# A transformer trunk on one core: the row-scaling after a transpose moves to one engine, and the weight ring grows by a slot

## The chip, the core and the metric

The kernel runs on one core of one Trainium2 chip. A core has a matrix engine (TensorE, PE in the profile), whose weight loads are listed apart (PEld), a vector engine (VectorE, DVE), an activation engine (ScalarE, ACT), a general engine (GpSimd, POOL) and a queue engine (SyncE, SP) that issues most transfers. Each engine works through its own instructions in order and waits on semaphores. The metric is the device time of one execution in microseconds, the median of the runs shown; lower is better.

## The reference

Two layers, each of three sub-layers on a sequence of 256 rows of width 1024, all in float32. Each sub-layer norms its input, scales and shifts it by vectors that come from a conditioning vector `c` (adaLN), and adds its gated result to `x`:

```python
for l in range(2):
    mod = silu(c) @ ada_w[l] + ada_b[l]               # 9 vectors of 1024
    sh1, sc1, g1, sh2, sc2, g2, sh3, sc3, g3 = split(mod, 9)
    h = rms_norm(x, norm_ffn1[l]) * (1 + sc1) + sh1
    x = x + 0.5 * g1 * swiglu(h, ffn1_w_in[l], ffn1_w_out[l])     # 1024 -> 2 x 2816 -> 1024
    h = rms_norm(x, norm_mix[l]) * (1 + sc2) + sh2
    x = x + g2 * token_mix(h, ...)                    # gMLP heads beside top-k attention heads
    h = rms_norm(x, norm_ffn2[l]) * (1 + sc3) + sh3
    x = x + 0.5 * g3 * swiglu(h, ffn2_w_in[l], ffn2_w_out[l])
return rms_norm(x, final_norm)
```

## The kernel before, in words

The 256 rows are two blocks of 128, b = 0 and b = 1. There are six phases in a row: ffn1, mix, ffn2 of layer 0, then of layer 1. The five borders between them are called T1 to T5 here, in order of time (T1: ffn1 to mix of layer 0; T2: mix to ffn2; T3: ffn2 to the next layer's ffn1; T4 and T5 as T1 and T2, in layer 1).

Every matrix product is made of three fp32r matmuls: each operand is split into a high part and the rest (`hi`, `lo`), and hi·hi, hi·lo and lo·hi are added up in a PSUM bank (`mm3`, L488). Weights come from HBM in pieces of 128x1024 float32 into a ring of `NRAW` raw tiles (`raw`, one SP transfer each). ScalarE then copies a piece to `whi` (L455), and VectorE subtracts that from the raw piece to make `wlo` (L456); `whi` and `wlo` live in a ring of `NB` slots. The function `pump` does this for the next piece of a fixed list; a slot is free again when block b = 1 has used it (`release`), a raw tile when its piece is converted. Between the weights stand pieces of `ada_w`, which are multiplied by `c` and added up in `aacc`: the first on ScalarE (L435), the others on VectorE (L440).

The program's order is fixed when the kernel is built: the Python code walks through the work in items (one weight piece for one block), and after each item runs deferred work and calls `pump`. Each engine's queue is that order. In a phase, block 0 is up to `LAG` = 6 items ahead of block 1. So at a border block 0 already multiplies for the new phase while block 1 ends the old one:

- Block 0's last products of the old phase are added to `x` (`update`, L539 and L541), squared and summed (L502), the root taken on POOL (L512), the rows scaled (L516), and, some items later, transposed on TensorE (L733) by `norm_T`.
- `norm_T` reads the transposed rows from PSUM, a bank of 4 tiles of 128x128 for each half h of the width, and applies scale A and shift B, which are per-partition columns after the transpose: one instruction a tile. Then `split` makes `hThi` (ScalarE, L534) and `hTlo` (VectorE, L535) of each half.
- Block 1 then goes the same way: its `update` stands on VectorE behind block 0's split and behind two weight conversions, and its transposes are placed after four items of block 0 in the new phase. TensorE waits there until block 1's rows are scaled (L516).

The lines around the change are

```python
if h < YH:
    S.activation(y[:, k, :], ps[:, q * P:(q + 1) * P], AF.Identity, bias=B, scale=A)      # L527
else:
    V.tensor_scalar(y[:, k, :], ps[:, q * P:(q + 1) * P], A, B, op0=ALU.mult, op1=ALU.add)  # L529
```

and, for both halves, `for fn in [norm_T(b, l2, i2, h) for h in range(2)]: fn()` (L556 to L558): both halves are scaled first, and then both are split.

In a mix phase, block 0's first product (`idx`) is taken from PSUM on ScalarE (L774), rotated on VectorE (`rope`, L696 to L701), one column block copied on ScalarE (L779) and transposed on TensorE (L733 on `idx`). Later `sgu_out` makes `u` on VectorE (L954), which TensorE transposes too. POOL loads two small tables of each layer by transfers that it issues itself; the one for the gMLP (L738, used at L745) is the largest.

Of the kernel before, what the change touches and what calls it, by code (L numbers as in the profile page):

```python
# [20 lines left out]
KF = DFF // P  # L21
DEPTH = 2
EPS = 1e-6
NB = 10
LEADJ = 8
LAG = 6
NRAW = 7
HOLD = 3
TAIL = 3
VX = 188  # L30
# [30 lines left out]
F1 = 62  # L61
ADA0_ACT = 1
COL_D = 2
YH = 1
TRL = 5
XPOS = 0
WLEAD = 0
# [30 lines left out]
def trunk(ctx, tc, x_in, c_in, pos_in, ada_w, ada_b, norm_ffn1, ffn1_w_in, ffn1_w_out,  # L98
# [6 lines left out]
    small = ctx.enter_context(tc.tile_pool(name="small", bufs=2))  # L105
    rawp = ctx.enter_context(tc.tile_pool(name="rawp", bufs=NRAW))
    hlp = ctx.enter_context(tc.tile_pool(name="hlp", bufs=NB))
    aap = ctx.enter_context(tc.tile_pool(name="aap", bufs=2))
# [201 lines left out]
    def defer(n, fn):  # L310
        pend.append([n, fn])
# [15 lines left out]
    def dma_fill():  # L327
        while dp[0] < len(seq):
# [5 lines left out]
            else:  # L334
                if n_r[0] - n_rd[0] >= NRAW:
                    break
# [75 lines left out]
    def pump(quota=2, force=False):  # L412
# [3 lines left out]
        while sp[0] < len(seq) and quota > 0:  # L416
# [8 lines left out]
            if e["k"] == "w" and not force and len(W) - wcur[0] >= lead[0]:  # L425
                break
            if need and r >= NB and not ring[r - NB]:
                assert not force, (r, ring[r - NB:], wcur, [q[0] for q in pend])
                break
# [36 lines left out]
    wcur = [0, 0]  # L466
    lead = [NB]

# [49 lines left out]
    def norm_T(b, l, i, h):  # L518
# [4 lines left out]
        for q in range(4):  # L523
            k = h * 4 + q
            A, B = ab[:, l, i - 1, 0, k:k + 1], ab[:, l, i - 1, 1, k:k + 1]
            if h < YH:
                S.activation(y[:, k, :], ps[:, q * P:(q + 1) * P], AF.Identity, bias=B, scale=A)  # L527
# [641 lines left out]
    for pi, (kind, l, i, n) in enumerate(phases):  # L1169
        with ExitStack() as es:  # L1170
# [28 lines left out]
            def both(stop):  # L1199
                while cnt[1] < stop:  # L1200
                    if cnt[0] < stop and cnt[0] - cnt[1] <= LAG:
                        item(0)
                        if pi == len(phases) - 1 and cnt[0] == n - 10:
                            fin_g[0] = vecp.tile([P, D], F32, name="vec", tag="vec")
                            nc.sync.dma_start(fin_g[0], bcast_row(final_norm, D))
                    else:
                        item(1)
            if kind == "f":
                both(n - KF)
                lead[0] = LEADJ  # L1210
                for q, _ in enumerate(joint_gen(env)):
# [6 lines left out]
                    if i == 1 and q == 4:  # L1218
                        sgu_prep(l, env)
                        sguT[l] = env["sgu_T"]  # L1220
                        defer(6, env["sgu_fin"])
                lead[0] = NB
            both(n)
# [29 lines left out]
```

## Time and profile before

| | us |
|---|---|
| median of 3 runs | 1018.31 (1015.11 to 1019.42) |
| the profiled execution's own time | 1017.07 |
| its span, first to last instruction | 1015.3 |
| TensorE busy | 983.5 (97%) |
| VectorE busy | 775.9 (76%) |
| ScalarE busy | 539.0 (53%) |
| POOL busy | 19.8 (2%) |

The chain of work that ended last is 84% TensorE, 9% VectorE, 3% ScalarE. The span is what the profile's views cover; the execution's own time is 1.77 us longer. A TensorE that is busy for a whole stretch can only be helped by fewer or shorter matmuls; where it stands idle, the row that follows names what it waited for. So the views to read are the waits of TensorE, and then, for each wait, the order of time on VectorE and ScalarE ahead of it.

### The profile page before, as it was taken

What the parts mean: (1) busy time and instruction counts of PE and PEld (TensorE: products, weight loads), DVE (VectorE), ACT (ScalarE), POOL (GpSimd) and SP (SyncE); (2) the same over time, 40 slices, a digit from 0 to 9 for tenths busy, and PEclk for the clock granted to TensorE, in tenths of its full rate; (3) what the DMA queues carried; (4) which work ended last, traced back from release to release, by engine and by line L of the source; (5) the groups of instructions that cost most, each with busy time, mean ns of one, the idle gap of its engine ahead of it and who ended that gap; (6) DMA issues with size and microseconds to landing.
All of it is one profiled execution on the core that took longest, in us unless ns stands there. A gap on an engine that the chain in (4) does not pass through costs nothing.

```text
span 1015.3 us, 16506 instructions
## 1 busy us (share of the span) xinstructions
PE 983.5 (97%) x6352; PEld 871.8 (86%) x6352; DVE 775.9 (76%) x1095; ACT 539.0 (53%) x832; POOL 19.8 (2%) x39
## 2 busy tenths in 40 slices
PE   5999999998999999999999999999999999999997
PEld 3699998887778799998878999987778879999886
DVE  3898988877997888887679798885879787566554
ACT  5575454446576645543456555534667766445341
POOL 4000000000000000000000000000000000000000
PEclk9999999999999999999999999999999999999999
DMA  9989899867664598878758899896555547665631
GB/s 328 340 309 339 316 380 346 317 203 230 192 188 146 168 346 313 313 273 289 273 161 289 341 330 353 320 343 193 157 147 156 154 146 259 250 218 188 217 116 42
DMA packets 109775, 253.40 MB, mean 250 GB/s; under 512 B 8499, under 2 KB 26981, under 8 KB 109697
## 3 DMA queue, kind: packets, MB, share of 16 engines
q1 hardware_dynamic: 108864, 251.20, 71.9%
q8 instruction: 50, 0.82, 0.3%
q0 software_dynamic: 544, 0.63, 0.2%
q10 hardware_dynamic: 288, 0.52, 0.1%
q14 instruction: 29, 0.23, 0.1%
HBM read 251.27 MB, written 1.05 MB: 249 GB/s over the span
## 4 chain that ended last, share of the span: by engine, by line
PE 84%; DVE 9%; ACT 3%; issue 2%; POOL 1%; DMA 1%; SPq 0%; POOLq 0%; ACTq 0%; DVEq 0%
PE bank L489 13%; PE bank L672 13%; PE bank L674 13%; PE bank L676 13%; PE bank L491 13%; PE bank L490 13%; PE bank L733 3%; DVE wlo L456 2%; DVE x L541 1%; ACT whi L455 1%; DVE xm L539 1%; PE bank L1047 1%; POOL rstd L512 1%; DVE aacc L1053 1%; DMA x<-in_x_dram 1%
## 5 line engine op out<-in xcount | busy, mean ns | idle before, releaser
L456 DVE TENSOR_TENSOR wlo<-raw,whi 128x1024 fp32r<-128x1024 f32 (+1 forms) x328 | 392.4, 1212 | 111.7 <-ACT whi L455 110.9
L455 ACT ACTIVATE whi<-raw 128x1024 fp32r<-128x1024 f32 (+1 forms) x328 | 334.4, 1045 | 217.4 <-PE bank L491 136.3
L672 PE MATMUL bank<-hThi,whi 128*128 128x256 f32 x1152 | 321.0, 279 | 0.0
L674 PE MATMUL bank<-hTlo,whi 128*128 128x256 f32 x1152 | 319.6, 277 | 0.0
L676 PE MATMUL bank<-hThi,wlo 128*128 128x256 f32 x1152 | 319.6, 277 | 0.0
L676 PEld LDWEIGHTS bank<-hThi,wlo 128*128 128x128 f32 x1152 | 217.6, 189 | 0.0
L672 PEld LDWEIGHTS bank<-hThi,whi 128*128 128x128 f32 x1152 | 216.3, 188 | 0.3
L674 PEld LDWEIGHTS bank<-hTlo,whi 128*128 128x128 f32 x1152 | 216.3, 188 | 0.3
L489 PE MATMUL bank<-whi,hThi 128*128 128x512 f32 (+1 forms) x384 | 154.5, 402 | 1.8 <-ACT hThi L1083 1.8
L491 PE MATMUL bank<-whi,hTlo 128*128 128x512 f32 (+1 forms) x384 | 149.0, 388 | 1.9 <-DVE hTlo L486 1.3
L490 PE MATMUL bank<-wlo,hThi 128*128 128x512 f32 (+1 forms) x384 | 147.6, 384 | 0.0
L440 DVE SCALAR_TENSOR_TENSOR aacc<-raw,ccol,aacc 128x1024 f32<-128x1024 f32 x112 | 143.1, 1278 | 0.0
L489 PE MATMUL bank<-whi,aThi 128*128 128x512 f32 (+1 forms) x374 | 142.3, 381 | 0.0
L490 PE MATMUL bank<-wlo,aThi 128*128 128x512 f32 (+1 forms) x374 | 141.2, 377 | 0.0
L491 PE MATMUL bank<-whi,aTlo 128*128 128x512 f32 (+1 forms) x374 | 141.0, 377 | 0.0
L489 PEld LDWEIGHTS bank<-whi,hThi 128*128 128x128 f32 x384 | 72.3, 188 | 19.8 <-issue 3.2
L491 PEld LDWEIGHTS bank<-whi,hTlo 128*128 128x128 f32 x384 | 72.1, 188 | 19.4 <-DVE hTlo L486 3.0
L490 PEld LDWEIGHTS bank<-wlo,hThi 128*128 128x128 f32 x384 | 72.3, 188 | 13.2 <-issue 0.5
L491 PEld LDWEIGHTS bank<-whi,aTlo 128*128 128x128 f32 x374 | 70.3, 188 | 13.3
L489 PEld LDWEIGHTS bank<-whi,aThi 128*128 128x128 f32 x374 | 70.4, 188 | 12.7
L490 PEld LDWEIGHTS bank<-wlo,aThi 128*128 128x128 f32 x374 | 70.4, 188 | 12.4
L681 ACT ACTIVATE xm<-bank 128x256 f32<-128x256 f32 x72 | 25.4, 379 | 62.5 <-PE bank L676 62.5
(150 smaller groups left out, 675.3 us busy)
## 6 DMA issues: line engine op xcount, KB each, us to landing
raw<-in_ffn_w_in_dram SPq DMA_DIRECT2D x176, 512.0 KB, 5.2
raw<-in_ada_w_dram SPq DMA_DIRECT2D x128, 512.0 KB, 5.7
raw<-in_ffn_w_out_dram SPq DMA_DIRECT2D x88, 512.0 KB, 5.3
raw<-in_mix_w_in_dram SPq DMA_DIRECT2D x40, 512.0 KB, 3.9
sraw<-in_ada_w_dram SPq DMA_DIRECT2D x32, 256.0 KB, 6.6
raw<-in_mix_w_out_dram SPq DMA_DIRECT2D x16, 512.0 KB, 3.6
vec<-in_ada_b_dram SPq DMA_DIRECT2D x6, 512.0 KB, 6.1
raw<-in_mix_w_in_dram SPq DMA_DIRECT2D x8, 324.0 KB, 3.0
```

The lines of the kernel that those rows point to most:

```text
L440: V.scalar_tensor_tensor(aacc, e["raw"], ccol[:, j:j + 1], aacc, op0=ALU.mult, op1=ALU.add)
L455: S.activation(hi[:, :n], src, AF.Copy)
L456: V.tensor_tensor(lo[:, :n], src, hi[:, :n].bitcast(F32), op=ALU.subtract)
L489: T.matmul(ps, ahi, whi, start=first, stop=False)
L490: T.matmul(ps, ahi, wlo, start=False, stop=False)
L491: T.matmul(ps, alo, whi, start=False, stop=last)
L512: G.tensor_tensor(r, ms, mhalf, op=ALU.pow)
L672: T.matmul(o, wh[:, kk, sl], ahi, start=first, stop=False, skip_group_check=True)
L674: T.matmul(o, wh[:, kk, sl], alo, start=False, stop=False, skip_group_check=True)
L676: T.matmul(o, wl[:, kk, sl], ahi, start=False, stop=k == KD - 1, skip_group_check=True)
L681: S.activation(a, acc[j][:, :256], AF.Silu)
L733: T.transpose(ps[:, i * P:(i + 1) * P], src(i), ident)
```

## The change: three constants and a smaller scratch

`YH` goes from 1 to 2, so that the second half's four tiles (L529 on VectorE) become four more of L527 on ScalarE, for each block at each of the five borders: 40 VectorE instructions become 40 of ScalarE. `NB` goes from 10 to 11 and `NRAW` from 7 to 8. The scratch that the software transfers of POOL use shrinks to 4096 bytes a partition, which pays for the two slot tiles and the raw tile.

```diff
-NB = 10
+NB = 11
-NRAW = 7
+NRAW = 8
-YH = 1
+YH = 2
-    nc = _bacc.Bacc("TRN2", target_bir_lowering=False, num_devices=1)
+    nc = _bacc.Bacc("TRN2", target_bir_lowering=False, num_devices=1,
+                     dynamic_dma_scratch_size=4096)
```

ScalarE's queue at T2, from the end of block 0's norm to block 1's squares: `xm_107` are block 0's rows, `xm_108` block 1's. Before:

```order
L455 ACTIVATE whi<-raw 128x1024 x2
L527 ACTIVATE xm_107<-bank_85,ab 128x128 x4
L534 ACTIVATE hThi<-xm_107 128x512 x2
L455 ACTIVATE whi<-raw 128x1024 x2
L502 ACTIVATE xm_108,ss<-x_106 128x512 x2
```

and with the change:

```order
L455 ACTIVATE whi<-raw 128x1024 x2
L527 ACTIVATE xm_107<-bank_85,ab 128x128 x4
L527 ACTIVATE xm_107<-bank_79,ab 128x128 x4
L534 ACTIVATE hThi<-xm_107 128x512 x2
L455 ACTIVATE whi<-raw 128x1024 x2
L502 ACTIVATE xm_108,ss<-x_106 128x512 x2
```

Four instructions have come in between the transposed rows and the two weight conversions behind them; nothing else has moved. VectorE's queue at the same place, from block 0's scaled rows to block 1's update, before:

```order
L516 TENSOR_SCALAR xm_107<-x_105,rstd 128x512 x2
L486 TENSOR_TENSOR hTlo<-bank_83,hThi 128x512
L456 TENSOR_TENSOR wlo<-raw,whi 128x1024 x2
L529 TENSOR_SCALAR xm_107<-bank_79,ab 128x128 x4
L535 TENSOR_TENSOR hTlo<-xm_107,hThi 128x512 x2
L456 TENSOR_TENSOR wlo<-raw,whi 128x1024 x2
L539 SCALAR_TENSOR_TENSOR xm_108<-bank_81,vec 128x512
```

and with the change:

```order
L516 TENSOR_SCALAR xm_107<-x_105,rstd 128x512 x2
L486 TENSOR_TENSOR hTlo<-bank_80,hThi 128x512
L456 TENSOR_TENSOR wlo<-raw,whi 128x1024 x2
L535 TENSOR_TENSOR hTlo<-xm_107,hThi 128x512 x2
L456 TENSOR_TENSOR wlo<-raw,whi 128x1024 x2
L539 SCALAR_TENSOR_TENSOR xm_108<-bank_82,vec 128x512
```

The row of L529 is gone; the two conversions ahead of block 1's update (L539) are still there. The other four borders read the same way on both engines. VectorE's queue at T1, from block 1's scaled rows to the rotation of block 0's `idx`, before:

```order
L516 TENSOR_SCALAR xm_108<-x_106,rstd 128x512 x2
L456 TENSOR_TENSOR wlo<-raw,whi 128x1024 x2
L529 TENSOR_SCALAR xm_108<-bank_82,ab 128x128 x4
L535 TENSOR_TENSOR hTlo<-xm_108,hThi 128x512 x2
L456 TENSOR_TENSOR wlo<-raw,whi 128x1024
L696 TENSOR_TENSOR rt<-idx,sinT 128x5x8
L698 TENSOR_TENSOR rt<-idx,sinT 128x5x8
L700 TENSOR_TENSOR idx<-idx,cosT 128x5x16
L701 TENSOR_TENSOR idx<-idx,rt 128x5x16
L440 SCALAR_TENSOR_TENSOR aacc<-raw,ccol,aacc 128x1024
```

and with the change:

```order
L516 TENSOR_SCALAR xm_108<-x_106,rstd 128x512 x2
L456 TENSOR_TENSOR wlo<-raw,whi 128x1024 x2
L535 TENSOR_TENSOR hTlo<-xm_108,hThi 128x512 x2
L440 SCALAR_TENSOR_TENSOR aacc<-raw,ccol,aacc 128x1024
L456 TENSOR_TENSOR wlo<-raw,whi 128x1024
L696 TENSOR_TENSOR rt<-idx,sinT 128x5x8
L698 TENSOR_TENSOR rt<-idx,sinT 128x5x8
L700 TENSOR_TENSOR idx<-idx,cosT 128x5x16
L701 TENSOR_TENSOR idx<-idx,rt 128x5x16
```

Besides the row of L529, one `ada_w` step (L440) has come from behind the rotation to ahead of it: with one slot and one raw tile more, the list is one piece further at every point. In the mix phase of layer 1 there are no `ada_w` pieces, and at T4 only the row of L529 goes. TensorE's rows around the five borders, are the same in both programs, and so is the order in which SP issues its transfers, but for the load of the last norm's weights, which comes one piece later.

## Rows read from the trace of the kernel before

**Rows 1.** Busy time of each engine in one stretch (start:end, length, PE, PEld, DVE, ...).

```profile
52.00:206.00 154.00, 154.00 (x1119) 144.90 (x1120) 135.91 (x172) 80.95 (x104) 0.00 (x0) 1.00 0.92 336
```

**Rows 2.** Waits of TensorE: who waited for whom, total us, times, longest.

```profile
PE bank L733 <- DVE xm L516: 14.0, 8, 3.6
...
PE bank L733 <- DVE u L954: 1.5, 1, 1.5
```

**Rows 3.** Timeline at T2: start, us, engine, line, what [idle before <- releaser].

```profile
331.07 1.51 ACT L527 ACTIVATE xm<-bank,ab 128x128 f32<-128x128 f32 x4 [1.81 <-PE bank L733]
...
332.61 1.16 ACT L534 ACTIVATE hThi<-xm 128x512 fp32r<-128x512 f32 x2
...
333.28 1.29 DVE L535 TENSOR_TENSOR hTlo<-xm,hThi 128x512 fp32r<-128x512 f32 x2 [0.38 <-ACT hThi L534]
...
333.67 1.99 ACT L455 ACTIVATE whi<-raw 128x1024 fp32r<-128x1024 f32 x2
...
334.75 2.36 DVE L456 TENSOR_TENSOR wlo<-raw,whi 128x1024 fp32r<-128x1024 f32 x2 [0.18 <-ACT whi L455]
...
341.50 0.88 DVE L516 TENSOR_SCALAR xm<-x,rstd 128x512 f32<-128x512 f32 x2 [0.73 <-POOL rstd L512]
```

**Rows 4.** Timeline at T1, block 0's scaling to block 1's transposes.

```profile
219.10 1.51 ACT L527 ACTIVATE xm<-bank,ab 128x128 f32<-128x128 f32 x4 [0.35 <-PE bank L733]
...
223.85 0.63 ACT L534 ACTIVATE hThi<-xm 128x512 fp32r<-128x512 f32 x1 [2.58 <-DVE xm L529]
224.39 1.99 ACT L455 ACTIVATE whi<-raw 128x1024 fp32r<-128x1024 f32 x2
...
232.69 1.09 PE L733 MATMUL bank<-ident,xm 128*128 128x128 f32 x8 [2.90 <-DVE xm L516]
```

**Rows 5.** Timeline at T3, ScalarE, block 0.

```profile
520.38 1.51 ACT L527 ACTIVATE xm<-bank,ab 128x128 f32<-128x128 f32 x4 [0.91 <-PE bank L733]
...
523.54 1.99 ACT L455 ACTIVATE whi<-raw 128x1024 fp32r<-128x1024 f32 x2
```

**Rows 6.** Timeline at T4, ScalarE, block 0.

```profile
711.44 1.51 ACT L527 ACTIVATE xm<-bank,ab 128x128 f32<-128x128 f32 x4 [0.32 <-PE bank L733]
...
715.21 1.99 ACT L455 ACTIVATE whi<-raw 128x1024 fp32r<-128x1024 f32 x2
```

**Rows 7.** Timeline at T5, ScalarE, block 0.

```profile
818.85 1.51 ACT L527 ACTIVATE xm<-bank,ab 128x128 f32<-128x128 f32 x4 [1.81 <-PE bank L733]
...
821.44 1.99 ACT L455 ACTIVATE whi<-raw 128x1024 fp32r<-128x1024 f32 x2
```

**Rows 8.** Timeline at T1, block 1's scaling to the transposes of block 0's idx.

```profile
234.07 1.48 ACT L527 ACTIVATE xm<-bank,ab 128x128 f32<-128x128 f32 x4
...
238.35 1.23 DVE L456 TENSOR_TENSOR wlo<-raw,whi 128x1024 fp32r<-128x1024 f32 x1 [0.26 <-ACT whi L455]
...
239.49 0.19 DVE L696 TENSOR_TENSOR rt<-idx,sinT 128x40 f32<-128x40 f32 x1
...
240.27 1.28 DVE L440 SCALAR_TENSOR_TENSOR aacc<-raw,ccol,aacc 128x1024 f32<-128x1024 f32 x1
...
240.50 0.58 PE L733 MATMUL bank<-ident,idx 128*128 128x128 f32 x3
```

**Rows 9.** Timeline at T4, the same place as Rows 8.

```profile
724.27 1.51 ACT L527 ACTIVATE xm<-bank,ab 128x128 f32<-128x128 f32 x4 [0.32 <-PE bank L733]
...
728.04 1.04 ACT L455 ACTIVATE whi<-raw 128x1024 fp32r<-128x1024 f32 x1
...
731.39 0.49 PE L733 MATMUL bank<-ident,idx 128*128 128x128 f32 x3
```

**Rows 10.** Timeline of VectorE in the first mix phase.

```profile
272.26 0.83 DVE L456 TENSOR_TENSOR wlo<-raw,whi 128x648 fp32r<-128x648 f32 x1 [0.96 <-ACT whi L455]
```

**Rows 11.** POOL's step on the gMLP table (timeline), and the table's use (min/median/max ns, first and last).

```profile
27.82 0.72 POOL L739 TENSOR_SCALAR_AFFINE_SELECT xm<-xm 128x512 f32<-128x512 f32 x1 [5.12 <-DMA xm<-in_sgu_w_dram]
...
L745 ACT ACTIVATE sguT<-bank x2: 599/599/599, 88.7 to 580.8; 128x512 f32<-128x512 f32 x2
```

## The prediction

> **What bounds the kernel now.** I read the waits of TensorE first. It is the engine that sets the time: in the stretch from 52 to 206 us it is busy for all of 154.00 us [rows 1], although the transfers take 0.92 of the 16 engines there. So nothing that only makes weights come sooner can pay in such a stretch. What is to be had lies in the waits. The largest group is TensorE at its transposes (L733), waiting for the rows that VectorE scales (L516): 14.0 us in 8 waits, the longest 3.6 [rows 2]; a smaller one is L733 behind `u`, 1.5 us once [rows 2].
>
> Then I read the timeline at each border backwards from such a wait. At T1 TensorE stood idle for 2.90 us before block 1's transposes [rows 4]. At T2 the reader can follow the whole path: ScalarE scales block 0's rows (331.07), splits both halves (332.61), then copies two weight pieces (333.67); VectorE subtracts those (334.75, 2.36 us), and only then comes to block 1's update and, at 341.50, to the scaled rows that TensorE waits for [rows 3]. So the path is: block 0's scaling, split, two conversions, block 1's update. From the first L455 on it holds the same instructions before and after; what the change touches is the interval from the first L527 to the first L455. A longer interval makes TensorE wait longer by as much, since it waits at every one of these borders already; a shorter one saves as much, up to the wait that is there (2.90 at T1).
>
> **The change part by part.**
>
> *Four more scalings on ScalarE, at block 0.* Four L527 take 1.54 us from start to the next instruction's start (331.07 to 332.61 [rows 3]). At T2 nothing of VectorE stands in the interval, since its own four are done before ScalarE's split comes, and the interval is 2.60 (331.07 to 333.67 [rows 3]). With four more it is 2.60 + 1.54 = 4.14, and with VectorE out of it, it should be 4.14 at all five borders:
>
> - T1: now 5.29 (219.10 to 224.39 [rows 4]), because ScalarE stands for 2.58 us until VectorE's four are done [rows 4]. Change: -1.15.
> - T2: now 2.60. Change: +1.54.
> - T3: now 3.16 (520.38 to 523.54 [rows 5]). Change: +0.98.
> - T4: now 3.77 (711.44 to 715.21 [rows 6]). Change: +0.37.
> - T5: now 2.59 (818.85 to 821.44 [rows 7]). Change: +1.55.
>
> Sum: +3.29 us. That ScalarE's second four cost what the first four did is the choice here; bounds follow below.
>
> *The same scaling at block 1.* It stands behind the wait, and TensorE goes on with block 0's items meanwhile. In a mix phase, though, the rotation of `idx` is queued behind it, and TensorE reaches the transposes of `idx` with no idle time now [rows 8, 9]. At T1: the first L527 at 234.07, the first split 1.54 + 1.54 later at 237.15, VectorE's pair L535 done 1.96 after that (332.61 to 333.28 + 1.29 [rows 3]) at 239.11. Now comes the step that has moved ahead, L440, 1.28 us [rows 8]: 240.39. The conversion takes 1.14 to the next instruction (238.35 to 239.49), and from there to the transposes are 1.01 (239.49 to 240.50 [rows 8]): 242.54, against 240.50, so 2.04 later; I take 0.1 off for slack that the rows don't show, +1.9. At T4 no L440 moves: the interval from L527 to L455 is 3.77 (724.27 to 728.04 [rows 9]) and becomes 4.14; +0.37 less slack, +0.2. Bounds: 0 if there is slack of that size after all, 2.04 and 0.37 if there is none. At T2, T3 and T5 I cost block 1's scaling at nothing: three items of block 0 stand between its transposes and its first product. If that cover is gone it is 1.54 each.
>
> *An `ada_w` step earlier in the first mix phase.* VectorE idles for 0.96 us at 272.26 for a conversion of 648 columns (0.83) [rows 10], and from there works without a gap to `u`. By the order of the changed program one more L440 lies ahead of that idle time, and between it and `u` there is one L440 (1.28 [rows 8]) and one 648-column conversion (0.83) less, and one full conversion (2.36 / 2 = 1.18 [rows 3]) more: -0.93. The L440 that moved fills the idle time and overruns it by 1.28 - 0.96 = 0.32. Net -0.6 of the 1.5 us wait [rows 2]. Bounds: 0 and -1.5.
>
> *Eleventh slot and eighth raw tile.* They convert one piece further ahead at every point, but no wait of TensorE for `whi` or `wlo` stands in its waits, and the two conversions ahead of block 1's update are still two. Zero, hidden by a TensorE that is fully busy [rows 1].
>
> *The smaller scratch.* Only POOL's transfers use it. The largest is in place at 27.82 and used at 88.7 [rows 11]: 60 us of cover, so zero. The trace can't show what a full scratch costs; beyond that cover it would delay TensorE one for one.
>
> Sum: 3.29 + 1.9 + 0.2 - 0.6 = +4.8 us on the profiled execution's own time of 1017.07 (span 1015.3 and 1.77 around it): 1021.9. The median shown is 1.24 above that execution; the runs differ by 4.3, and I stay with 1022.
>
> *A rule against the rows.* The rows say 0.385 us for a 128-column scaling on ScalarE (1.54 / 4 [rows 3]). The Trainium skill, page "VectorE: DVE Perf Modes", section "The TRN2 errata — SBUF-src ops pay a fixed extra latency per instruction", gives ScalarE 172 cycles plus one per column from PSUM at 1.2 GHz; that is, as an estimate from that page, 300 / 1.2 = 250 ns, and 258 ns for VectorE. By that price the added four would cost 1.0 instead of 1.54, at five borders and at T1's `idx`, about 3.4 us less in the sum: +1.4. The rows decide here; the page's price is too low for this instruction.
>
> **The rivals.**
>
> *ScalarE takes the four in its idle time (the faster side).* For it: ScalarE is idle for 2.58 us at T1 just there [rows 4], and VectorE is the busier engine. If the added four cost nothing, the intervals change by -2.69, 0, -0.56, -1.17 and 0 = -4.4, `idx` by 2.04 - 1.54 - 0.1 = +0.4, `u` by -0.6: -4.6, 1012.5. Against: at T2 and T5 the interval has no idle time to give [rows 3, 7]. It decides at -4.4 + 0.4 - 0.6 + 6c = 0, where four cost c = 0.77, 0.19 us a tile, half of what they do in every row. A part of it, between 1014 and 1019, is likelier than the whole: a tile at 0.27 us (c = 1.08) instead of 0.385 would give 4.8 - 6 x 0.46 = +2.0, 1019.1. The page's price above lies on this rival's way too; as every row of L527 speaks against it, it gets 0.04.
>
> *The slot pays.* If the eleventh slot took the two conversions from ahead of block 1's update, each border would save up to 2.36 [rows 3], 11.8 in all within the 14.0 of waits [rows 2]: 1010. Against: the order still has both there at all five.
>
> *Block 1's split becomes the wait (slower).* If block 0's three items don't cover it, T2, T3 and T5 add up to 1.54 each: +4.6 more, 1026.5. It decides at a slack under 1.54 us. The waits show none for block 1 now, and its second four on VectorE are late already, so part of that slack is proven.
>
> *Nothing moves.* If the waits take all up, 1017 to 1018.
>
> **How the numbers follow.** About 0.5%, 5.1 us, is what a measurement of this kernel can tell from no change; the sum lies just inside. My forecast (1019.5 to 1024.5): 0.52, of which 0.20 over the bound. Block 1's split: 0.18, slower. Part or all of the added steps hidden, with nothing moving and the page's price among it: 0.22, of which 0.03 faster. The slot pays: 0.08, faster. So faster 0.11, same 0.51, slower 0.38. The range, 1014 to 1026.5, leaves out the slot's case, the cheapest end of ScalarE's and little above.
>
> **What would show it.** In the profile after: the interval from first L527 to first L455 at 4.1 us at all five borders; TensorE's wait for L516 shorter at T1 by about 1.1 and longer at T2 and T5 by about 1.5; a new wait at L733 for `idx` of nearly 2 us at T1; the wait for `u` near 0.9; no wait for POOL. I am wrong if the intervals come out unequal, if the conversions behind them wait for slots or raw tiles, or if TensorE waits for block 1's `hThi` at T2, T3 or T5.

## The result: slower by 0.57%, and where the microseconds are

The changed kernel takes 1023.02 us (median of 16 runs, 1020.09 to 1027.51), the kernel before, on the same chip, 1018.15 (16 runs, 1014.94 to 1020.95). The ratio is 1.0057, with a 95% interval of 1.004 to 1.0073. So it is slower by 4.9 us, and the forecast was 1022.0. The profiled execution has a span of 1020.3 us, where the sum had 1020.1. That the total fits doesn't say that its terms do: some were too large, and one was not in the sum at all.

The first part of the page of the changed kernel, busy time by engine (us, share, instructions):

```profile
PE 985.5 (97%) x6352; PEld 873.6 (86%) x6352; DVE 760.9 (75%) x1055; ACT 548.3 (54%) x872; POOL 19.6 (2%) x39
```

VectorE has given up 40 instructions and 15 us of work, ScalarE has taken 40 and 9 us, and the span is 5.0 us longer. Sums by engine don't decide here; the waits do. The waits of TensorE in the changed kernel (who for whom, total us, times, longest):

```profile
PE bank L733 <- DVE xm L516: 16.9, 8, 3.6
...
PE bank L733 <- DVE u L954: 1.4, 2, 1.2
...
PE bank L733 <- DVE idx L701: 1.2, 1, 1.2
```

Against [rows 2] the wait for the scaled rows has grown by 2.9 us in total (0.5 of it at 12 us, long ahead of the first border), a wait for `idx` has come, as forecast, and `u` is 0.1 shorter in all. That is 4.0 us more, less some 1.2 in small waits of before that are gone (0.4 for block 0's `hTlo` at T1, 0.8 for the first `hThi`, near the start). A wait for block 1's `hThi`, which one rival had, and a wait for POOL are not there.

The timeline of the changed kernel at the five borders: at T1 block 0, then block 1's transposes and the way to those of `idx`; at T2 block 0's path to its end; the first scaling and first conversion of block 0 at T3, T4 and T5.

```profile
219.52 2.90 ACT L527 ACTIVATE xm<-bank,ab 128x128 f32<-128x128 f32 x8 [0.36 <-PE bank L733]
...
223.31 2.04 ACT L455 ACTIVATE whi<-raw 128x1024 fp32r<-128x1024 f32 x2
...
231.67 1.09 PE L733 MATMUL bank<-ident,xm 128*128 128x128 f32 x8 [2.15 <-DVE xm L516]
...
237.69 1.28 DVE L440 SCALAR_TENSOR_TENSOR aacc<-raw,ccol,aacc 128x1024 f32<-128x1024 f32 x1
...
241.03 0.58 PE L733 MATMUL bank<-ident,idx 128*128 128x128 f32 x3 [1.23 <-DVE idx L701]
...
331.00 2.90 ACT L527 ACTIVATE xm<-bank,ab 128x128 f32<-128x128 f32 x8 [1.80 <-PE bank L733]
...
333.75 1.19 ACT L534 ACTIVATE hThi<-xm 128x512 fp32r<-128x512 f32 x2
...
334.79 2.04 ACT L455 ACTIVATE whi<-raw 128x1024 fp32r<-128x1024 f32 x2
...
342.66 0.88 DVE L516 TENSOR_SCALAR xm<-x,rstd 128x512 f32<-128x512 f32 x2 [0.73 <-POOL rstd L512]
...
343.21 1.97 PE L733 MATMUL bank<-ident,xm 128*128 128x128 f32 x8 [2.19 <-DVE xm L516]
...
523.07 2.90 ACT L527 ACTIVATE xm<-bank,ab 128x128 f32<-128x128 f32 x8 [0.91 <-PE bank L733]
...
526.86 2.04 ACT L455 ACTIVATE whi<-raw 128x1024 fp32r<-128x1024 f32 x2
...
714.80 2.90 ACT L527 ACTIVATE xm<-bank,ab 128x128 f32<-128x128 f32 x8 [0.33 <-PE bank L733]
...
718.60 2.03 ACT L455 ACTIVATE whi<-raw 128x1024 fp32r<-128x1024 f32 x2
...
822.61 2.90 ACT L527 ACTIVATE xm<-bank,ab 128x128 f32<-128x128 f32 x8 [1.81 <-PE bank L733]
...
826.40 2.04 ACT L455 ACTIVATE whi<-raw 128x1024 fp32r<-128x1024 f32 x2
```

Subtract the first start of L527 from that of L455: 3.79, 3.79, 3.79, 3.80 and 3.79 us. The interval is the same at all five borders, as forecast, but 0.35 shorter than the 4.14 that the sum took. Against before it is 1.50 shorter at T1 [rows 4], and 1.19, 0.63, 0.03 and 1.20 longer at T2 to T5 [rows 3, 5 to 7]. TensorE's wait for block 1's rows is 2.15 at T1, where it was 2.90 [rows 4], so only half of T1's gain shows there (0.4 more is the wait for `hTlo` that has gone); at T2 it is 2.19, where it was 0.94.

The row at 343.21 shows something else: eight transposes take 1.97 us there, and 1.09 at T1. The windows view, three stretches of 3 us or less around that place in the changed kernel (length, PE busy and so on; the figure before the DMA share is the granted clock of TensorE):

```profile
337.00:340.00 3.00, 3.00 (x15) 2.46 (x14) 2.96 (x5) 0.36 (x1) 0.00 (x0) 1.00 0.56 180
343.00:346.00 3.00, 2.79 (x11) 2.60 (x12) 2.82 (x4) 2.22 (x6) 0.00 (x0) 0.50 0.12 22
347.00:350.00 3.00, 3.00 (x14) 2.44 (x13) 2.02 (x3) 2.24 (x4) 0.00 (x0) 1.00 0.69 222
```

The same stretch in the kernel before:

```profile
343.00:346.00 3.00, 3.00 (x16) 2.45 (x15) 3.00 (x7) 1.91 (x6) 0.00 (x0) 1.00 0.44 111
```

Behind the wait at T2 TensorE runs at 0.50 of its clock in the changed kernel, and at 1.00 before, where the profile has no such place between its start and its end. What it costs can be read from the rows of the transposes of block 1 at T2 and of both blocks at T3, before:

```profile
342.04 1.09 PE L733 MATMUL bank<-ident,xm 128*128 128x128 f32 x8 [0.94 <-DVE xm L516]
...
519.74 1.03 PE L733 MATMUL bank<-ident,xm 128*128 128x128 f32 x8
...
531.91 1.09 PE L733 MATMUL bank<-ident,xm 128*128 128x128 f32 x8 [1.55 <-DVE xm L516]
```

and in the changed kernel, behind the row at 343.21:

```profile
522.43 1.03 PE L733 MATMUL bank<-ident,xm 128*128 128x128 f32 x8
...
535.27 1.09 PE L733 MATMUL bank<-ident,xm 128*128 128x128 f32 x8 [2.21 <-DVE xm L516]
```

From T2 to T3 the changed kernel needs 192.06 us (343.21 to 535.27), the kernel before 189.87 (342.04 to 531.91). Of the 2.19 more, 0.66 is the wait at T3, which grew from 1.55 to 2.21; the other 1.5 us is the clock.

Cut at the starts of such transposes, TensorE's rows add up all of the 5.0 us between the two profiles (us):

| stretch of TensorE | before | after | difference |
|---|---|---|---|
| start to block 0's transposes at T1 | 218.46 | 218.88 | +0.42 |
| block 0's to block 1's transposes, at T1 | 14.23 | 12.79 | -1.44 |
| at T2 | 11.61 | 12.85 | +1.24 |
| at T3 | 12.17 | 12.84 | +0.67 |
| at T4 | 12.84 | 12.90 | +0.06 |
| at T5 | 11.60 | 12.84 | +1.24 |
| block 1's transposes at T1 to those of `idx` | 7.81 | 9.36 | +1.55 |
| from there to block 0's at T2 (the rest of the mix phase, with `u`) | 89.93 | 89.33 | -0.60 |
| block 1's at T2 to block 0's at T3 (with the stretch at half clock) | 177.70 | 179.22 | +1.52 |
| block 1's at T4 to block 0's at T5 (the second mix phase) | 94.63 | 94.96 | +0.33 |
| block 1's at T3 to block 0's at T4, and block 1's at T5 to the end | 364.32 | 364.33 | +0.01 |

So in these two executions the path costs 1.77 at the borders, and 1.77 + 1.55 - 0.60 + 0.33 = 3.05 us in all; the clock costs 1.5, and 0.4 stands ahead of T1. (A stretch can grow by more than its wait row says, because the row counts idle time from the modelled end of the matmul before: 1.55 against 1.23 for `idx`.)

So two theories stood at this point. Mine: the path to block 1's update costs 2 to 3 us, the step ahead of `idx` is part of that, and the rest is TensorE's clock, which falls behind the longer waits. The rivals: the slot and its order carry the cost; or the scaling costs all of it by itself, and the clock falls by chance, whatever the waits are.

### The profile page after: what moved, and what is told of

Same layout as the page of the kernel before. It is cut to its first block, busy times and chain, and to the rows that moved or that the text cites. A ratio compares the mean times of both kernels' runs of the same rounds, so it can differ in the third digit from the quotient of the medians.

```text
span 1020.3 us, 16487 instructions
## 1 busy us (share of the span) xinstructions
PE 985.5 (97%) x6352; PEld 873.6 (86%) x6352; DVE 760.9 (75%) x1055; ACT 548.3 (54%) x872; POOL 19.6 (2%) x39
## 4 chain that ended last, share of the span: by engine, by line
PE 81%; DVE 8%; ACT 5%; issue 2%; DMA 2%; SPq 1%; POOL 0%; POOLq 0%; ACTq 0%; DVEq 0%
PE bank L672 13%; PE bank L676 13%; PE bank L674 13%; PE bank L489 13%; PE bank L491 12%; PE bank L490 12%; PE bank L733 3%; DVE wlo L456 2%; ACT xm L527 2%; ACT whi L455 2%; DVE x L541 1%; DMA sraw<-in_ada_w_dram 1%; DVE xm L539 1%; DMA raw<-in_ffn_w_in_dram 1%; PE bank L1047 1%
## 5 line engine op out<-in xcount | busy, mean ns | idle before, releaser
L455 ACT ACTIVATE whi<-raw 128x1024 fp32r<-128x1024 f32 (+1 forms) x328 | 332.7, 1046 | 177.7 <-PE bank L491 127.9
L440 DVE SCALAR_TENSOR_TENSOR aacc<-raw,ccol,aacc 128x1024 f32<-128x1024 f32 x112 | 143.0, 1277 | 0.0
```

The source lines that it names most:

```text
L440: V.scalar_tensor_tensor(aacc, e["raw"], ccol[:, j:j + 1], aacc, op0=ALU.mult, op1=ALU.add)
L455: S.activation(hi[:, :n], src, AF.Copy)
```

## The experiments

**The two halves of the change, apart.** The first run keeps `YH` at 1:

```diff
-YH = 2
+YH = 1
```

> The slot, the raw tile and the scratch alone; block 0's second half is scaled on VectorE as before. My theory: the intervals from the first L527 to the first L455 read as before (5.3, 2.6, 3.2, 3.8, 2.6 us at T1 to T5), one ada_w step stands ahead of the rotation of idx, so TensorE waits about 1.2 us more at the transposes of idx at T1, and about 0.3 us less for u; TensorE's clock is granted in full behind T2, whose wait stays under 1 us. Sum: +0.9 us on 1018.2, 1019.1. Rival 'the slots cost it all': 1022 to 1023, with waits for whi, wlo or raw that were not there. Rival 'the slots cost nothing': 1018.2, no wait for idx.

It took 1017.84 us, against 1018.59 for the kernel before (ratio 0.9989, 0.9978 to 1.0), so my 1019.1 is a miss. The slots cost nothing, and the rival that they cost it all is out. But the clock is not what I expected. TensorE's rows behind T1's wait and behind T4's in this run, and windows there:

```profile
232.53 1.97 PE L733 MATMUL bank<-ident,xm 128*128 128x128 f32 x8 [2.92 <-DVE xm L516]
...
723.68 1.94 PE L733 MATMUL bank<-ident,xm 128*128 128x128 f32 x8 [2.14 <-DVE xm L516]
```

```profile
232.50:235.50 3.00, 2.97 (x11) 2.76 (x12) 2.78 (x4) 2.97 (x7) 0.00 (x0) 0.50 0.63 182
...
723.90:726.90 3.00, 3.00 (x12) 2.71 (x12) 3.00 (x6) 2.22 (x6) 0.00 (x0) 0.50 0.19 31
```

T1 and T4 are the two borders where TensorE waits over 2 us in this run (2.92 and 2.14), as before (2.90 and 2.11), and in this execution both waits were followed by half clock. The profiled execution of before had neither. The wait for `idx` that I expected was not there: with TensorE slow behind T1, `idx` was in time.

The second run takes the kernel before with `YH` at 2.

```diff
-YH = 1
+YH = 2
```

> The four scalings a block alone, with ten slots, seven raw tiles and the scratch as before. My theory: the interval from the first L527 to the first L455 is 3.8 us at all five borders, TensorE's wait for the scaled rows is 2.2 us at each, no wait for idx at T1 above 0.3 us. The five borders add up to -1.25 + 1.2 + 0.65 + 0.1 + 1.2 = +1.9 us, 1020.1, or 1021.6 if a stretch at half clock follows T2 as in the profile of the change. Rival 'the scaling costs it all': 1022 to 1023 without such a stretch. Rival 'ScalarE does it for nothing': 1018.2 or less.

1022.93 us (ratio 1.0044, 1.003 to 1.0058): the move of the scalings alone takes as long as the whole change. That is above both my numbers, and it is the time of the rival "the scaling costs it all", though that rival had no stretch at half clock. Its waits and its windows show what that time is made of: waits of TensorE,

```profile
PE bank L733 <- DVE xm L516: 15.7, 8, 3.6
...
PE bank L733 <- DVE idx L701: 0.3, 1, 0.3
```

and the windows behind T1, T2 and T5:

```profile
230.50:233.50 3.00, 3.00 (x18) 2.62 (x18) 2.53 (x3) 3.00 (x8) 0.00 (x0) 1.00 0.52 140
342.00:345.00 3.00, 3.00 (x12) 2.61 (x11) 2.19 (x2) 2.56 (x8) 0.00 (x0) 0.50 0.27 71
833.60:836.60 3.00, 3.00 (x11) 2.52 (x10) 2.04 (x2) 2.79 (x9) 0.00 (x0) 0.50 0.34 91
```

All five border waits are 2.13 to 2.22 us here, and two of them were followed by half clock. Taking this with the runs above: the half clock always stands behind one of these waits, but not behind each.

**TensorE kept busy in the waits.** To tell the clock from the path, this run puts eight matmuls into each of block 1's waits in the changed kernel (`norm_T`; they write the bank that the transposes then overwrite):

```diff
-        ps = transposes(lambda q: xm[b][:, (h * 4 + q) * P:(h * 4 + q + 1) * P], 4)
+        ps = tp_tile()
+        if b == 1 and h == 0:
+            for _ in range(FILL):
+                T.matmul(ps, ones, hT[0][0][:, 0:4, :], start=True, stop=True)
+        for q in range(4):
+            T.transpose(ps[:, q * P:(q + 1) * P], xm[b][:, (h * 4 + q) * P:(h * 4 + q + 1) * P], ident)
```

> The change, with eight further matmuls of 512 columns ahead of block 1's transposes at each border (they write the bank that the transposes then overwrite, 8 times 0.227 us = 1.8 us of the 2.2 us wait). Theory that the half clock behind T2 comes from TensorE's idle time there: no stretch at half clock after the start, and about 1.5 us less than the change alone wherever that had one; 1021.0 to 1022.5 as a median. Theory that the half clock comes by chance and not from the wait: stretches at half clock still stand behind one border or another, and the time is that of the change, 1023. If the eight matmuls don't fit in the wait, the time rises by what they overrun, under 1 us a border.

1019.75 us, 3.3 less than the change, with more matmuls in it. The runs lie between 1019.21 and 1020.64, a spread of 1.4 us instead of 7.4, and the profile has no half clock between the start and the end: behind T2, where the change had it, this run's window reads

```profile
342.50:345.50 3.00, 3.00 (x18) 2.62 (x19) 2.60 (x3) 2.69 (x8) 0.00 (x0) 1.00 0.18 38
```

The mean granted clock is 0.9953 over these 11 runs and 0.9916 over the 16 of the change. So the half clock comes from the idle time at the border and not by chance; the profiles of the three filled versions below have none there either. The gain is larger than I expected. Nine of the 16 runs of the change have a lower granted clock than the profiled one, so they may well have had more than its one stretch; no trace of them shows it.

With the same matmuls in the waits of the other three versions, the path can be compared at equal clock. In the two whose waits differ from border to border the number of matmuls follows them (10, 4, 6, 8 and 4 at T1 to T5). The kernel before:

> The kernel before, with further matmuls ahead of block 1's transposes that stay within its own waits (10, 4, 6, 8 and 4 of 0.227 us at T1 to T5). Theory (the half clock comes from TensorE's long waits, and each stretch costs about 1.7 us): no stretch at half clock between the start and the end, every run near the profiled one that had none, 1017.0 us, with a spread of under 2.5 us instead of 4.8; against the change with its waits filled (1019.75) that leaves 2.7 us for the path alone, and the rest of the 4.9 us by which the change was slower, 2.2, is clock. Rival (the filled matmuls win nothing here, the clock of before was never touched): 1018.6, spread as before, and the path is all of the difference.

1016.60 us, with a spread of 2.25 and no half clock between the start and the end of its profile, as the theory had it. The slot, the raw tile and the scratch alone:

> The slot, the raw tile and the scratch alone, with the same filled waits. Theory: no stretch at half clock; the profiled run without the filling had two of them and a span of 1017.3, so 1017.3 - 2 x 1.7 + 1.8 = 1015.7 us, 1.3 less than the kernel before with filled waits. Rival (the slots are worth nothing at equal clock): 1017.0, as the kernel before with filled waits.

1016.70: my 1015.7 is a miss, and the rival holds. At full clock the slots are worth nothing. That is a sum of parts: against the profile of the run before, TensorE's stretch at T1 is 0.6 us shorter and the rest of the first mix phase 0.6, but the way to `idx` is 1.0 longer and the second mix phase 0.3. Where their `ada_w` step went is seen in this run's waits, which e1_slots_only hid (the added lines move L733 to L738 and L701 to L706):

```profile
PE bank L738 <- DVE idx L706: 0.9, 1, 0.9
```

The scalings alone:

> The four scalings a block alone (ten slots, seven raw tiles), with eight further matmuls in each wait as in e3_filled. Theory (the move costs the same path with and without the slot; idx is 0.45 later instead of 1.4): no stretch at half clock, 1019.75 - 0.9 = 1018.8 us, 2.2 above the kernel before with filled waits (1016.6). Rival (the slot is what makes the move dear, by the ada_w step ahead of idx): 1017.5 or less. Rival (the slot makes the move cheaper): 1020 or more.

1018.96, as forecast. The four numbers:

| waits filled | scaling on both engines | scaling on ScalarE |
|---|---|---|
| 10 slots, 7 raw tiles | 1016.60 | 1018.96 |
| 11 slots, 8 raw tiles | 1016.70 | 1019.75 |

By these medians the move costs 2.4 us with the old ring and 3.05 with the new one. But the four versions ran on three chips, and by their ratios to the kernel before on the same chip the move costs 0.26% and 0.24%, which is 2.6 and 2.4 us, so that the times don't tell the two apart. The `ada_w` step ahead of `idx` adds nothing to the move itself: in the profiles the way to `idx` grows by 0.6 with the old ring and 0.5 with the new one. Together the change costs 3.15 at equal clock, of 4.9 without the matmuls; the other 1.7 us is clock. The intervals allow for more: the ratio to the kernel before is 1.0011 (1.0003 to 1.002) for the change with filled waits and 0.9988 (0.9977 to 0.9998) for the kernel before with them, 0.23%, which is 2.3 us. The granted clock gives a rough third estimate of the clock's share: its mean is 0.9940 over 23 runs of the kernel before (0.9942 and 0.9949 in two later sets) and 0.9916 over 16 runs of the change, and 0.0024 of 1020 us is 2.4 us. So the path costs 2.3 to 3.2 us, and the clock 1.7 to 2.6; the table of TensorE's stretches, with 3.05 and 1.5 in one execution of each, fits that.

**Is it the path, or the instructions?** If the scalings cost only because a wait of TensorE stands behind them, they must cost nothing when the path is short. The first attempt to shorten it holds the conversions back for 7 items instead of 3, with the scaling on both engines and the slot, the raw tile and the small scratch:

```diff
-HOLD = 3
+HOLD = 7
```

> The slot, the raw tile and the scratch, the scaling on both engines as before, and the number of items without a conversion after the end of block 0's phase raised from 3 to 7, so that the two conversions leave the place ahead of block 1's update and stand behind block 1's split. Theory of the path (scaling, split, two conversions, update, squares, scaled rows): two conversions on ScalarE and the VectorE subtraction of up to 2.4 us leave it, the waits of TensorE for the scaled rows vanish at T2, T3 and T5 and shrink to under 1 us at T1 and T4, 1010 to 1014 in all, if the ring of eleven covers five conversions that come late; a TensorE that waits for whi or wlo in the items behind would show where it doesn't, up to 1.2 us a border, 1014 to 1018. Rival 'the wait is not set by the conversions': the waits for the scaled rows stay at 0.9 to 2.9 and the time at 1018 to 1020.

1043.11 us (ratio 1.024, 1.0224 to 1.0256), a miss by 30 us. The waits of TensorE:

```profile
PE bank L489 <- ACT whi L455: 16.4, 5, 3.3
PE bank L733 <- DVE xm L516: 5.5, 3, 3.6
PE bank L490 <- DVE wlo L456: 5.4, 8, 1.1
```

The waits for the scaled rows did vanish at all five borders for block 1 (the 5.5 us that are left stand near the start and at block 0 of T4, as before), so the two conversions were on the path. But the pieces are needed right behind the transposes: the five new waits for `whi`, each of about 3.3 us, are longer than the old ones, and all five are followed by half clock. What is wanted is a later place, not a much later one. So the next runs stop the conversions from block 0's split to the end of block 1's phase, and go on with them one or two items behind that, ahead of block 1's split:

```diff
-HOLD = 3
+HOLD, HOLD1 = 3, 2
...
-            hold[0] = HOLD
+            hold[0] = HOLD if b == 0 else HOLD1
...
                 for fn in [norm_T(b, l2, i2, h) for h in range(2)]:
                     fn()
+                if b == 0:
+                    hold[0] = 1 << 20
```

With `HOLD1` at 1:

> The slot, the raw tile and the scratch with the scaling on both engines, and block 0's split no longer followed by two conversions: nothing is converted from there to the end of block 1's phase, and four pieces directly behind block 1's squares (on VectorE behind its scaled rows). My theory of the path: the waits of TensorE for the scaled rows lose 2.0 to 2.4 us each (3.1, 1.1, 1.7, 2.3, 1.1 become about 0.9, 0, 0, 0.1, 0), 8 us in all, and none of them is long enough to be followed by a half clock: 1018.2 - 0.7 - 8 = 1009 to 1011. Rival (the conversions are needed where they stand): waits for whi or wlo appear behind the transposes and take back 1 us or more at each border, 1014 to 1019.

1012.94 us (ratio 0.995, 0.9933 to 0.9968). The waits for block 1's scaled rows are gone at T2 to T5, as forecast, but four conversions ahead of block 1's split make TensorE wait for `idx`, `hTlo` and `hThi` (2.0, 1.8 and 0.2 us), so the time is above the theory's range. With `HOLD1` at 2:

> As the run before, but the conversions begin one item later, so that three instead of four stand ahead of block 1's scaling. Theory: the same gain of the waits, 1009 to 1011, and idx at T1 is not late; if TensorE uses up its pieces in the pause, a wait for whi or wlo of up to 1 us a border, more than in the run before: up to 1015.

1008.62 us (0.9908, 0.9891 to 0.9926), a little under the forecast, though `idx` is still late, by 0.6 us at T1 and at T4. The timeline of that run at T2:

```profile
330.11 1.16 ACT L534 ACTIVATE hThi<-xm 128x512 fp32r<-128x512 f32 x2
330.77 1.29 DVE L535 TENSOR_TENSOR hTlo<-xm,hThi 128x512 fp32r<-128x512 f32 x2 [0.39 <-ACT hThi L534]
331.99 0.68 DVE L539 SCALAR_TENSOR_TENSOR xm<-bank,vec 128x512 f32<-128x512 f32 x1
...
336.46 0.88 DVE L516 TENSOR_SCALAR xm<-x,rstd 128x512 f32<-128x512 f32 x2 [0.73 <-POOL rstd L512]
337.26 3.49 DVE L456 TENSOR_TENSOR wlo<-raw,whi 128x1024 fp32r<-128x1024 f32 x3
338.42 1.04 PE L735 MATMUL bank<-ident,xm 128*128 128x128 f32 x8
```

Block 1's update (L539) follows block 0's split at once, the scaled rows are there 1.0 us before TensorE comes to them, and the conversions lie behind. (The added lines move L733 to L735 here.) Now the change's scalings were put into this version:

> The run e8_late_2 with the four scalings a block moved to ScalarE as in the change, and nothing else. My theory (the move costs only where the interval to block 0's split stands ahead of a wait): in e8_late_2 the scaled rows of block 1 are ready 1.0, 0.7 and 1.0 us before TensorE comes to them at T2, T3 and T5, so the interval of 3.8 us everywhere (1.2, 0.65 and 1.2 more there, 1.25 less at T1) costs 0.2, 0 and 0.2, gains 0.5 at T1, and idx may come 0.5 later: 1008.6 to 1009.6 us, where the same move cost 4.9 in the change (3.1 of it with filled waits). Rival (ScalarE or the four instructions are dearer in themselves, wherever they stand): 2 to 3 us, 1011 to 1012.

1007.56 us (0.9912, 0.9896 to 0.9928 against the kernel before; e8_late_2 has 0.9908). The move that cost 4.9 us as part of the change costs nothing that these ratios can tell; that is a little less than I had allowed for. Its timeline at T2 shows the same 2.75 us from the first scaling to the split as in the change, and no wait:

```profile
326.81 2.90 ACT L527 ACTIVATE xm<-bank,ab 128x128 f32<-128x128 f32 x8 [1.81 <-PE bank L735]
329.56 1.19 ACT L534 ACTIVATE hThi<-xm 128x512 fp32r<-128x512 f32 x2
...
335.94 0.88 DVE L516 TENSOR_SCALAR xm<-x,rstd 128x512 f32<-128x512 f32 x2 [0.73 <-POOL rstd L512]
336.67 1.04 PE L735 MATMUL bank<-ident,xm 128*128 128x128 f32 x8
```

So the cost is that of the place, not of the instruction. Two more runs belong to this version. Without the slot, the raw tile and the small scratch:

> The run e8_late_2 without the eleventh slot, the eighth raw tile and the smaller scratch. Theory that the gain of e8_late_2 is the place of the conversions alone: 1008 to 1010. Theory that the pause in the conversions needs the further slot to be bridged: waits for whi or wlo at three or more borders, 1011 to 1016.

1010.52 us (0.994, 0.9927 to 0.9954), a little above the first theory's range. Here TensorE waits 2.2 us for `idx` instead of 1.1; waits for `wlo` are 0.2 in all, so the pause does not need the slot, though the order that comes with it suits this version better, by 2 to 3 us (1.9 by the medians, 0.32% by the ratios). And one conversion less ahead of `idx`:

> The run e8_late_2, with the conversions one item later still at T1 and T4 alone, so that two instead of three stand ahead of block 1's scaling there and the rotation of idx comes 1.2 us earlier. Theory: the two waits for idx (0.7 and 0.7 us) vanish and nothing else moves, 1007.2 to 1007.8. Rival (the pieces run out): a wait for whi or wlo takes their place, 1008.6 or more.

1007.96 us (0.9914, 0.9899 to 0.9929), the same as without it. The wait for `idx` at T4 went, that at T1 stayed (0.7 us, 0.6 without it), and a new one of 0.7 came for ScalarE's copy of the next columns (L776), so its forecast fell.

## Why the forecast came out right, and which of its terms were wrong

**The mechanism** held: the interval from first scaling to first conversion is equal at all five borders, ScalarE had no idle time to give at T2 and T5, the gain at T1 is there, and the loss goes into TensorE's waits, with no wait for POOL, for slots, or for block 1's split.

**The price of four scalings** was too high. From the first L527 to L534 eight take 2.75 us (331.00 to 333.75), so the next four cost 1.2, not the 1.54 that I carried over from the first four [rows 3]. With eight in a row the tiles follow each other at 0.34 us, and four of those are 0.16 less than the 1.54. I take the 0.16 for a hand-over: before, the split of the first half reads what the fourth scaling has just written; with eight, the first split's data are long there. Only these rows speak for that. The Trainium skill, page "ScalarE: Activation LUTs", section "What ACT_TABLE_LOAD costs", has 186 ns plus 0.833 a column, 93 more for each pointer operand, and an overlap of 93 between neighbours. For 128 columns with scale and bias as pointers that is, as an estimate from that page, 186 + 107 + 186 - 93 = 386 ns from start to start; the rows lie 11% below it, and a good third above the 250 ns that I had weighed against them. With the measured intervals the borders add up to -1.50 + 1.19 + 0.63 + 0.03 + 1.20 = +1.55, and TensorE's stretches there to +1.77, where the sum had +3.29. With `idx` and `u` below that makes 3.05, within the 2.3 to 3.2 of the runs with filled waits.

**`idx` at T1** was forecast at +1.9, and TensorE's stretch to it grew by 1.55 (1.23 of that in the wait's row). The step ahead of it was priced nearly rightly, at 1.28; but block 1's eight scalings are about as much shorter as block 0's. At T4 it was forecast at +0.2, and the stretch is 7.81 us in both profiles. **`u`** was forecast at -0.6, and the rest of the first mix phase is 0.60 shorter, though the wait itself lost only 0.3; but a new wait for `u`, of 0.15, stands in the second mix phase, which is 0.33 longer, and the sum had no term for that. **Slot and scratch** at zero: at equal clock 1016.70 against 1016.60 says so, if their `ada_w` step is counted with them.

**The step that failed** is the sentence "a longer interval makes TensorE wait longer by as much", taken as the whole price of a wait. The sum had no term for what the wait does to TensorE's clock, though the kernel before already had two such waits (2.90 at T1 [rows 4], 2.11 at T4) and a spread of 4.3 us between three runs that I left unexplained. That the total came out is luck: in the profiles the terms were 1.5 us too large at the borders and 0.55 at `idx`, 2.1 together, and what the sum left out was 1.5 of clock, 0.3 in the second mix phase and 0.4 ahead of T1, 2.3 together. The rival "ScalarE takes the four in its idle time" fell with 1018.96 against 1016.60; "the slot pays" fell with 1016.70, though a version in which the conversions do leave their place comes to 1008.62, about where that rival had it (1010). "Nothing moves" fell with the interval of the ratio.

## What to carry to other kernels

Before moving work from a busy engine to an idle one, ask which of the two stands ahead of the wait that counts: here the idle engine's next instruction was the path's next step, and the busy engine had no need of relief. Look then for what stands on that path without belonging to it: moving two weight conversions gained 10 us with the new ring and 7 with the old one (8 and 6 against the same rings with filled waits, so a part of it is clock), the four scalings cost 2 to 3, and once the conversions had moved, the scalings could stand on either engine. Where a kernel's runs spread by more than a change is worth, look for stretches of lower clock behind TensorE's waits, and compare versions with those waits filled.

## What the runs showed of the hardware that was not expected

TensorE's granted clock fell to 0.50 (1.2 instead of 2.4 GHz) behind border waits of 2.1 to 2.9 us, in some executions and not in others: behind none of two such waits in the profile of the kernel before, one of five in the change, two of two with the slots alone, two of five with the scalings alone; behind the 3.3 us waits of e4_hold7_slots it fell five times of five. In this case's profiles no such stretch stands behind a border wait that matmuls had filled (four profiles), and none in the versions whose border waits are all under 1 us. A stretch at half clock behind such a wait cost 1.5 us in the change and 1.6 in e1_slots_only: for the second value, e1_slots_only needs 9.43 us from T4's transposes of block 1 to those of `idx` (723.68 to 733.11) and the kernel before 7.81 (723.58 to 731.39). The Trainium skill, page "TensorE: Matmul & The Clock Gate", section "What's actually happening", names 1.2 and 2.4 GHz as the two states of this clock. The rows agree (0.50 or 1.00). Matmuls whose result is thrown away took 3.3 us off the change and 1.8 off the kernel before. Why one wait is followed by a lower clock, and the next of the same length is not, stays open.

One more thing stays open: four of the 16 runs of the change have spans of 1024.8 to 1025.0 us, two of them at a granted clock of 0.992 that explains less than that; no profile was taken of such a run.
